# One layer of a streaming encoder: weights converted two tiles ahead, a norm's last squares summed on TensorE, a Silu behind the norm's statistics

## The chip, the cores and the metric

The kernel runs on one core of one Trainium2 chip. The core has five engines, each with a queue of its own that it works through strictly in order: TensorE (PE in the profile) for matmuls, VectorE (DVE), ScalarE (ACT), GpSimd (POOL) and SyncE (SP), which here only issues DMA transfers. They meet at semaphores. The metric is the device time of one execution in microseconds (us), lower is better. About 0.2% of it (some 3.5 us) is what a measurement of this kernel can tell from no change.

## What is computed

One layer of a hybrid encoder over 1024 new frames of one stream and 64 of another, width 1024, all in float32. Cut to what matters here (`x` is the residual stream, `mix` the result of the two head groups, `mod` six vectors made from a conditioning vector):

```python
mod = jax.nn.silu(c) @ w_ada + b_ada
sh1, sc1, gt1, sh2, sc2, gt2 = jnp.split(mod, 6, axis=-1)
...
mix = jnp.concatenate([y_rwkv, y_fox], axis=-1) @ w_out
x = x + gt1[:, None] * mix
h2 = _rms_norm(x, norm2_g) * (1 + sc2[:, None]) + sh2[:, None]
ffn = (jax.nn.silu(h2 @ w_ffn_gate) * (h2 @ w_ffn_up)) @ w_ffn_down
x = x + gt2[:, None] * ffn
```

`_rms_norm` divides by the root of the mean square over the 1024 columns of a frame.

## The kernel before

Activations lie with features on the 128 partitions and frames along the free axis, so a vector of 1024 features is 8 tiles (`KT`). Frames are split into two halves: half 0 has 512 frames, half 1 has 576 (512 and the 64 of the second stream), which is worked in two chunks of 288 columns. Each float32 product is made of three matmuls: weights and activations are each split into a rounded high part and a low rest (`whi`, `wlo`), and high by high, low by high and high by low are summed (`mm3`, L294 to L296).

A weight tile takes four steps: a DMA into one of four raw buffers (`raw_w`, L282), a cast to the high part on ScalarE (L212), a subtraction for the low part on VectorE (L216), and its matmuls. There are two buffers each for the high and the low part, so tile o+2 can be cast only when the matmuls of tile o are over.

The stage that the change touches is the stretch from the end of the attention to the first block of the feed-forward network, in `run`:

- The **output projection of half 1** (`outproj`): for each of 8 tiles o, 48 matmuls into the PSUM tile `po` (24 for each chunk), and VectorE adds the gated result to the residual `x1` (`add_gated`, L1002; three instructions for a tile, of 288, 224 and 64 columns, since the last chunk holds both streams).
- Behind each tile `x1_sq`: a DMA of the tile to a scratch tensor (L1008), its squares on ScalarE (L1010, into `nsq`, two buffers), and the sum with the squares so far on VectorE (L1012). At the end `x1_rs` sums over partitions with a matmul against ones (L1022, PSUM tile `pn2`) and forms the reciprocal root as Ln and Exp on ScalarE (L1025, L1026, into `nrs`).
- In between the tiles stand the steps of `h2_make` for half 0, a generator: the norm itself (L1050 on VectorE, L1052 on ScalarE), and the seven sums and differences of blocks of `h2` (L1054, L1055; `hh` and `hl`) that a Strassen-like feed-forward with seven products instead of eight needs. From o = 4 the first gate weights are loaded, at o = 5 prepared in the same way (`fast_prep`, L1096, L1100, L1106: `hS1` to `hS4`, `hA22` and their low parts).
- Then `x1_rs` of half 1, four tiles of the conditioning product (`ada_run`: 8 matmuls `pada`, a copy `mrow` on ScalarE, a transposing matmul, two small VectorE instructions each), and the feed-forward (`ffn`), whose first block runs the gate product of half 0 (`pfa`, `pfb`, `pfc`, `pfe` against `hh0`, 84 matmuls of 256 columns), with the steps of `h2_make` of half 1 between them, and then that of half 1 (against `hh1`). Its results go through Silu on ScalarE (L1198).

Code order is not the order on an engine. The kernel is written for a framework that lists each engine's instructions by a priority that follows the code, advances an instruction where its operands come free by its own reckoning, and adds the semaphores. A table of functions must be loaded on ScalarE (ACT_TABLE_LOAD) where the next function isn't in the loaded one; the loads are put in by the order of the instructions. The waits of an instruction hold up all that stands behind it on its engine.

Of the kernel before, what the change touches and what calls it, by code (L numbers as in the profile page):

```python
# [10 lines left out]
AF = mybir.ActivationFunctionType  # L11
# [5 lines left out]
P = 128  # L17
D = 1024
KT = D // P
# [45 lines left out]
class K:  # L65
# [938 lines left out]

    def x1_sq(self, hf, o, acc):

        nc, n = self.nc, hf.n
        nc.sync.dma_start(self.x1scr[hf.i][:, o], self.x1[hf.i][:, o, 0:n])  # L1008
        sq = self.slot(name="nsq", tag="hs")
        nc.scalar.activation(sq[:, 0:n], self.x1[hf.i][:, o, 0:n], AF.Square)  # L1010
        if acc is not None:
            nc.vector.tensor_tensor(sq[:, 0:n], sq[:, 0:n], acc[:, 0:n], op=ALU.add)  # L1012
        return sq

    def x1_rs(self, hf, acc):

        nc, n = self.nc, hf.n
        rs = self.slot(name="nrs", tag="rs")
        sums = []
        for off, m in hf.chunks:  # L1020
            ps = self.ps([P, 512], tag="b", name="pn2")
            nc.tensor.matmul(ps[:, 0:m], self.ones, acc[:, off:off + m], start=True, stop=True)  # L1022
            sums.append(ps)
        for a, (off, m) in zip(sums, hf.chunks):
            nc.scalar.activation(rs[:, off:off + m], a[:, 0:m], AF.Ln, scale=1.0 / D, bias=self.eps_n)  # L1025
        nc.scalar.activation(rs[:, 0:n], rs[:, 0:n], AF.Exp, scale=-0.5)  # L1026
        return rs
# [142 lines left out]
    def ffn(self, halves, raw, w, h2gen, gap, early, mid):  # L1170
# [3 lines left out]
        nc, A = self.nc, self.A  # L1174
# [3 lines left out]
        for i in range(len(src)):  # L1178
# [8 lines left out]
            for hf in halves:  # L1187
                n = hf.n // 2

                def out(q, ps, u):  # L1190
                    if not up:
# [3 lines left out]
                        if u is not None:  # L1195
                            nc.vector.tensor_tensor(d, ps, u, op=ALU.add)
                            ps = d
                        nc.scalar.activation(d, ps, AF.Silu)  # L1198
                        return
# [132 lines left out]
    def run(self):  # L1332
        tc, nc, A, O = self.tc, self.nc, self.A, self.O
        halves = [Half(0), Half(1)]
        with ExitStack() as top:
# [167 lines left out]
            acc = None  # L1503
            for o in range(KT):
                acc = self.x1_sq(halves[0], o, acc)
            w1 = [self.load_w(A["w_out"][o], [P, KT, P]) for o in range(2)]
            h2 = self.h2_make(halves[0], self.x1_rs(halves[0], acc))
            pair = lambda x: [A[x][i] for i in range(2)]
            acc, raw, w, ada = None, [], {}, []
            for o in range(KT):  # L1510
                self.outproj(halves[1], o, ("ab", "ce")[o % 2], w1[o] if o < 2 else None)
                acc = self.x1_sq(halves[1], o, acc)
                next(h2, None)
                if o in (0, 2):
                    next(h2, None)
# [7 lines left out]
            ada = [(t, self.ada_load(t)) for t in range(40, 44)]  # L1523
            rs = self.x1_rs(halves[1], acc)

# [176 lines left out]
```

## Time and profile before

| | us |
|---|---|
| time, median of 3 runs | 1743.63 |
| lowest and highest run | 1741.31, 1744.07 |
| the profiled execution's own time | 1735.94 |
| its span, first to last instruction | 1734.2 |
| PE busy in the span | 1663.8 (96%) |
| DVE busy | 1126.6 (65%) |
| ACT busy | 729.1 (42%) |

The mean granted TensorE clock is 0.981. All stretches below are of this one execution, in us from the first instruction: the output projection of half 1 lies at 925 to 988, the first block of the feed-forward from there to about 1045. In rows of the timeline stand start, duration, engine, source line, operation, written tile and read tiles, shape, how many instructions were merged, and in brackets the idle time of the engine just before it with what ended it. Durations of successive matmuls overlap; what a matmul costs is the distance of starts.

### The profile page before, as it was taken

How to read it: one execution, taken by the hardware profiler on the slowest of the kernel's cores; microseconds unless marked ns; L12 is line 12 of the kernel's file. 1: busy time of each engine (PE TensorE's matmuls, PEld its weight loads, DVE VectorE, ACT ScalarE, POOL GpSimd, SP SyncE). 2: the span in 40 equal slices, each digit the busy share in tenths (PEclk: the TensorE clock that was granted, in tenths of full speed). 3: DMA queues.
4: the chain of work that ended last, by engine and by line, in shares of the span. 5: the costliest groups of instructions: out<-in, count | busy, mean ns of one | idle time of the engine just before them, and what ended most of it. 6: DMA issues, size and time to landing. Idle time of an engine off the chain costs nothing.

```text
span 1734.2 us, 33257 instructions
## 1 busy us (share of the span) xinstructions
PE 1663.8 (96%) x12893; PEld 1447.9 (83%) x12893; DVE 1126.6 (65%) x2574; ACT 729.1 (42%) x1532; POOL 180.8 (10%) x412
## 2 busy tenths in 40 slices
PE   5999999999999999889999989999999999999999
PEld 3676766688888888766888889999999999999998
DVE  6676676757686753876877686666666655555545
ACT  4534454553454445765776453333233223211210
POOL 2102121131221212300210000000000000000000
PEclk9999999999899999989999999999999999999999
DMA  8535457632233344566553333222222224433213
GB/s 314 149 95 137 142 140 207 175 93 56 55 76 75 95 121 136 157 194 177 151 177 136 127 115 101 75 75 75 76 75 82 78 87 143 161 98 98 95 37 122
DMA packets 133581, 207.09 MB, mean 119 GB/s; under 512 B 62126, under 2 KB 70350, under 8 KB 133422
## 3 DMA queue, kind: packets, MB, share of 16 engines
q1 hardware_dynamic: 133422, 204.95, 39.3%
q8 instruction: 102, 1.67, 0.4%
q14 instruction: 57, 0.47, 0.1%
HBM read 157.65 MB, written 47.25 MB: 118 GB/s over the span
## 4 chain that ended last, share of the span: by engine, by line
PE 82%; DVE 7%; ACT 7%; DMA 2%; issue 2%; SPq 1%; POOL 0%; DVEq 0%; ACTq 0%; POOLq 0%
PE pd L1264 15%; PE pfc L1153 8%; PE pfe L1153 8%; PE pfa L1153 7%; PE pmm L294 5%; PE pmm L296 5%; PE pmm L295 5%; PE pfb L1153 4%; PE pav L962 2%; PE pbs L375 2%; PE pA L464 2%; PE ppt L940 2%; PE po L294 1%; PE po L295 1%; PE po L296 1%
## 5 line engine op out<-in xcount | busy, mean ns | idle before, releaser
L294 PE MATMUL pmm<-hhi,whi 128*128 128x288 f32 (+1 forms) x624 | 220.7, 354 | 0.7 <-ACT pb L317 0.7
L295 PE MATMUL pmm<-hlo,whi 128*128 128x288 f32 (+1 forms) x624 | 218.2, 350 | 0.0
L296 PE MATMUL pmm<-hhi,wlo 128*128 128x288 f32 (+1 forms) x624 | 218.0, 349 | 0.0
L212 ACT CAST whi<-wraw 128x1024 fp32r<-128x1024 f32 (+2 forms) x116 | 99.3, 856 | 214.4 <-PE pd L1264 167.0
L1264 PE MATMUL pd<-ah,wlo 128*128 128x512 f32 (+1 forms) x528 | 173.5, 329 | 0.0
L1264 PE MATMUL pd<-al,whi 128*128 128x512 f32 (+1 forms) x528 | 173.2, 328 | 0.0
L1264 PE MATMUL pd<-ah,whi 128*128 128x512 f32 (+1 forms) x528 | 173.0, 328 | 0.0
L1268 DVE SCALAR_TENSOR_TENSOR x1t<-pd,mod,x1t 128x512 f32<-128x512 f32 x192 | 91.4, 498 | 110.6 <-PE pd L1264 110.0
L294 PEld LDWEIGHTS pmm<-hhi,whi 128*128 128x128 f32 x624 | 120.3, 193 | 13.5 <-ACT pb L317 2.0
L296 PEld LDWEIGHTS pmm<-hhi,wlo 128*128 128x128 f32 x624 | 120.3, 193 | 10.9 <-issue 1.7
L295 PEld LDWEIGHTS pmm<-hlo,whi 128*128 128x128 f32 x624 | 120.4, 193 | 9.6 <-issue 0.7
L216 DVE TENSOR_TENSOR wlo<-wraw,whi 128x1024 fp32r<-128x1024 f32 (+2 forms) x108 | 103.8, 961 | 26.0 <-ACT whi L212 25.6
L1153 PE MATMUL pfc<-hh,hS 128*128 128x256 f32 (+1 forms) x352 | 102.0, 290 | 4.4 <-ACT hh L1055 4.4
L1264 PEld LDWEIGHTS pd<-al,whi 128*128 128x128 f32 x528 | 99.4, 188 | 7.7
L1264 PEld LDWEIGHTS pd<-ah,whi 128*128 128x128 f32 x528 | 99.3, 188 | 7.7
L1264 PEld LDWEIGHTS pd<-ah,wlo 128*128 128x128 f32 x528 | 99.2, 188 | 7.4
L1153 PE MATMUL pfc<-hl,hS 128*128 128x256 f32 (+1 forms) x352 | 102.3, 290 | 0.0
L1153 PE MATMUL pfc<-hh,lS 128*128 128x256 f32 (+1 forms) x352 | 102.0, 290 | 0.0
L1153 PE MATMUL pfa<-hl,whi 128*128 128x256 f32 (+1 forms) x352 | 101.8, 289 | 0.0
L1153 PE MATMUL pfa<-hh,whi 128*128 128x256 f32 (+1 forms) x352 | 101.7, 289 | 0.0
L1153 PE MATMUL pfa<-hh,wlo 128*128 128x256 f32 (+1 forms) x352 | 101.4, 289 | 0.0
L604 POOL TENSOR_SCALAR sd<-sv,pc 64x64 f32<-64x64 f32 x136 | 72.0, 529 | 172.9 <-DVE sv L617 156.6
(360 smaller groups left out, 4402.0 us busy)
## 6 DMA issues: line engine op xcount, KB each, us to landing
wraw<-in_w_in_dram SPq DMA_DIRECT2D x52, 512.0 KB
wada<-in_w_ada_dram SPq DMA_DIRECT2D x48, 512.0 KB
as<-actscr SPq DMA_DIRECT2D x22, 544.0 KB
wraw<-in_w_gate_dram SPq DMA_DIRECT2D x22, 512.0 KB
wraw<-in_w_up_dram SPq DMA_DIRECT2D x22, 512.0 KB
wraw<-in_w_down_dram SPq DMA_DIRECT2D x40, 256.0 KB
wraw<-in_w_out_dram SPq DMA_DIRECT2D x16, 512.0 KB
actscr<-sg SPq DMA_DIRECT2D x22, 288.0 KB
```

The source lines that it names most:

```text
L212: nc.scalar.copy(hi, src)
L216: eng.tensor_tensor(lo, src, hi.bitcast(F32), op=ALU.subtract)
L294: nc.tensor.matmul(ps[0:M, 0:n], whi[:, k, 0:M], xhi[:, k, off:off + n], start=(k == 0), stop=False)
L295: nc.tensor.matmul(ps[0:M, 0:n], whi[:, k, 0:M], xlo[:, k, off:off + n], start=False, stop=False)
L296: nc.tensor.matmul(ps[0:M, 0:n], wlo[:, k, 0:M], xhi[:, k, off:off + n], start=False, stop=(k == kt - 1))
L375: nc.tensor.matmul(ps[:, 0:n], w, x[:, off:off + n], start=True, stop=True)
L464: nc.tensor.matmul(pa[h][:, i], kb[hp, c + i], rk[hp, c + i], start=True, stop=True)
L604: nc.gpsimd.tensor_scalar(sd[hsl[h]], sv[hsl[h], c, h], pc[hsl[h], c], None, op0=ALU.mult)
L940: nc.tensor.transpose(pt[0:rows, b - b0, t * P:t * P + qn], p[0:qn, pc:pc + rows], self.ident[0:qn, 0:qn])
L1153: nc.tensor.matmul(ps, l[:, k], r[:, s, k], start=(first and k == 0 and y == 0), stop=(k == 3 and y == 2), skip_group_check=True)
L1264: nc.tensor.matmul(ps[:, 0:n], w[:, i], x[:, t:t + n], start=(i == 0 and y == 0), stop=(i == len(fs) - 1 and y == 2))
L1268: nc.vector.scalar_tensor_tensor(dst, ps[:, so - off:so - off + l], self.mod[:, 40 + o, b:b + 1], dst, op0=ALU.mult, op1=ALU.add)
```

## The change

Five things are changed in the stretch above; what is computed stays the same.

1. In half 1's projection the raw load, cast and subtraction of tile o+2 are issued right behind tile o, ahead of the norm's steps of half 0 that follow; before, tile o converted its own weights when its turn came (tiles 0 and 1 excepted).
2. Half 0's statistics and its first norm steps stand behind tile 1 instead of ahead of tile 0.
3. The squares of the last tile are made chunk by chunk and are not added to the sum on VectorE: `x1_rs` takes the sum of seven tiles and the last squares, and adds them up in PSUM, with two matmuls for each chunk.
4. The DMA of the last tile to scratch stands behind its squares in the code.
5. The Silus of the first gate block (`i == 0`, four for each half) are issued after the Exp of half 1's statistics.

```diff
-    def x1_sq(self, hf, o, acc):
+    def x1_sq(self, hf, o, acc, last=False):
         nc, n = self.nc, hf.n
+        sq = self.slot(name="nsq", tag="hs")
+        if last:
+            for off, m in hf.chunks:
+                nc.scalar.activation(sq[:, off:off + m], self.x1[hf.i][:, o, off:off + m], AF.Square)
         nc.sync.dma_start(self.x1scr[hf.i][:, o], self.x1[hf.i][:, o, 0:n])
-        sq = self.slot(name="nsq", tag="hs")
+        if last:
+            return sq
...
-    def x1_rs(self, hf, acc):
+    def x1_rs(self, hf, *accs):
...
-            nc.tensor.matmul(ps[:, 0:m], self.ones, acc[:, off:off + m], start=True, stop=True)
+            for i, acc in enumerate(accs):
+                nc.tensor.matmul(ps[:, 0:m], self.ones, acc[:, off:off + m], start=(i == 0), stop=(i == len(accs) - 1))
...
-        nc.scalar.activation(rs[:, 0:n], rs[:, 0:n], AF.Exp, scale=-0.5)
+        self.rs_done = nc.scalar.activation(rs[:, 0:n], rs[:, 0:n], AF.Exp, scale=-0.5)
...
-                        nc.scalar.activation(d, ps, AF.Silu)
+                        if i == 0:
+                            with self.tc.issue_after(self.rs_done.ins):
+                                nc.scalar.activation(d, ps, AF.Silu)
+                        else:
+                            nc.scalar.activation(d, ps, AF.Silu)
...
-            h2 = self.h2_make(halves[0], self.x1_rs(halves[0], acc))
+            acc0 = acc
...
-                self.outproj(halves[1], o, ("ab", "ce")[o % 2], w1[o] if o < 2 else None)
-                acc = self.x1_sq(halves[1], o, acc)
-                next(h2, None)
-                if o in (0, 2):
+                self.outproj(halves[1], o, ("ab", "ce")[o % 2], w1[o])
+                if o == KT - 1:
+                    sq = self.x1_sq(halves[1], o, None, True)
+                else:
+                    acc = self.x1_sq(halves[1], o, acc)
+                if o + 2 < KT:
+                    w1.append(self.load_w(A["w_out"][o + 2], [P, KT, P]))
+                if o == 1:
+                    h2 = self.h2_make(halves[0], self.x1_rs(halves[0], acc0))
+                    next(h2, None)
+                    next(h2, None)
+                if o:
+                    next(h2, None)
+                if o == 2:
                     next(h2, None)
...
-            rs = self.x1_rs(halves[1], acc)
+            rs = self.x1_rs(halves[1], acc, sq)
```

How this moves instructions is seen at three places. The first is VectorE's queue around the low part of the fourth weight tile (o = 3), `wlo_11848` before; `hl0` and `x1_0` belong to half 0's norm, `po` to the projection, `nsq` to the sum of squares. Before:

```order
L1002 SCALAR_TENSOR_TENSOR x1_1_11590<-po_11779,mod_160,x1_1_11590 128x288
L1012 TENSOR_TENSOR nsq_11765<-nsq_11765,nsq_11700 128x576
L1054 TENSOR_TENSOR hl0_11586<-x1_0_9536,hh0_11585 128x1024
L1050 SCALAR_TENSOR_TENSOR x1_0_9536<-x1_0_9536,g2_162,nrs_11641 128x512
L1054 TENSOR_TENSOR x1_0_9536<-x1_0_9536 128x4x256
L1002 SCALAR_TENSOR_TENSOR x1_1_11590<-po_11805,mod_160,x1_1_11590 128x224
L1002 SCALAR_TENSOR_TENSOR x1_1_11590<-po_11805,mod_160,x1_1_11590 128x64
L1054 TENSOR_TENSOR x1_0_9536<-x1_0_9536 128x4x256
L216 TENSOR_TENSOR wlo_11848<-wraw_11845,whi_11847 128x1024
```

After, where the same tile's low part is called `wlo_11763`:

```order
L1018 TENSOR_TENSOR nsq_11625<-nsq_11625,nsq_11621 128x512
L1002 SCALAR_TENSOR_TENSOR x1_1_11590<-po_11729,mod_160,x1_1_11590 128x224
L1002 SCALAR_TENSOR_TENSOR x1_1_11590<-po_11729,mod_160,x1_1_11590 128x64
L216 TENSOR_TENSOR wlo_11763<-wraw_11760,whi_11762 128x1024
L1018 TENSOR_TENSOR nsq_11756<-nsq_11756,nsq_11694 128x576
L1057 SCALAR_TENSOR_TENSOR x1_0_9536<-x1_0_9536,g2_162,nrs_11766 128x512 x6
L1002 SCALAR_TENSOR_TENSOR x1_1_11590<-po_11785,mod_160,x1_1_11590 128x288
```

The subtraction stood behind the evictions of tile 2 (`po_11779`, `po_11805`) and all eight norm steps; now it stands behind the eviction of tile 1 (`po_11729`) and ahead of all of them. On TensorE the matmuls of tiles 0 to 7 now follow each other with only half 0's `pn2` between; before, 18 of the 84 matmuls of the feed-forward's first product (`pfa`, `pfc`) stood among those of tiles 6 and 7.

The second place is ScalarE's queue at the end of the projection: the squares of the last tile (`nsq`), the norm's Ln and Exp (`nrs`), the first Silu (`sg`). Before:

```order
L1010 ACTIVATE nsq_12200<-x1_1_11590 128x576
L1198 ACT_TABLE_LOAD
L1198 ACTIVATE sg_12360<-pfa_12295 128x256
L1025 ACT_TABLE_LOAD
L1025 ACTIVATE nrs_12211<-pn2_12212,eps_n_154 128x288
L1025 ACTIVATE nrs_12211<-pn2_12214,eps_n_154 128x288
L1026 ACT_TABLE_LOAD
L1026 ACTIVATE nrs_12211<-nrs_12211 128x576
L193 COPY mrow_12228<-pada_12219 128x128
```

After:

```order
L1012 ACTIVATE nsq_12199<-x1_1_11590 128x288
L1107 CAST hS2_12071<-wraw_11991 128x512
L1032 ACTIVATE nrs_12211<-pn2_12212,eps_n_154 128x288
L1107 CAST hS4_12079<-wraw_11989 128x512
L193 COPY mrow_12230<-pada_12221 128x128
L1012 ACTIVATE nsq_12199<-x1_1_11590 128x288
L1032 ACTIVATE nrs_12211<-pn2_12215,eps_n_154 128x288
L1033 ACTIVATE nrs_12211<-nrs_12211 128x576
L193 COPY mrow_12241<-pada_12232 128x128
L1164 COPY fu_12310<-pfa_12297 128x256
```

Three table loads and a Silu are gone from between squares and Exp; the whole program has five table loads before and two after, the second of them now for the first Silu, 15 rows behind the Exp. Two casts of the gate's weights (`hS2`, `hS4`) and a copy of the conditioning product (`mrow`) have come in.

The third place is VectorE's queue at the same time. Before:

```order
L216 TENSOR_TENSOR wlo_12143<-wraw_12140,whi_12142 128x1024
L1012 TENSOR_TENSOR nsq_12135<-nsq_12135,nsq_12041 128x576
L1002 SCALAR_TENSOR_TENSOR x1_1_11590<-po_12146,mod_160,x1_1_11590 128x288
L1002 SCALAR_TENSOR_TENSOR x1_1_11590<-po_12172,mod_160,x1_1_11590 128x224
L1002 SCALAR_TENSOR_TENSOR x1_1_11590<-po_12172,mod_160,x1_1_11590 128x64
L1012 TENSOR_TENSOR nsq_12200<-nsq_12200,nsq_12135 128x576
L1050 SCALAR_TENSOR_TENSOR x1_1_11590<-x1_1_11590,g2_162,nrs_12211 128x512
```

After:

```order
L1002 SCALAR_TENSOR_TENSOR x1_1_11590<-po_12146,mod_160,x1_1_11590 128x288
L1103 TENSOR_TENSOR wraw_11991<-wraw_11991,wraw_11989 128x512
L1002 SCALAR_TENSOR_TENSOR x1_1_11590<-po_12172,mod_160,x1_1_11590 128x224
L1103 TENSOR_TENSOR wraw_11989<-wraw_11989,wraw_11991 128x512
L1103 TENSOR_TENSOR lS2_12072<-wraw_11991,hS2_12071 128x512
L1002 SCALAR_TENSOR_TENSOR x1_1_11590<-po_12172,mod_160,x1_1_11590 128x64
L1103 TENSOR_TENSOR lS4_12080<-wraw_11989,hS4_12079 128x512
L200 TENSOR_REDUCE mred_12244<-pada_12221 128x2
L201 TENSOR_SCALAR mod_160<-mred_12244,vc_135 128x2
L1057 SCALAR_TENSOR_TENSOR x1_1_11590<-x1_1_11590,g2_162,nrs_12211 128x512
```

The sum of the last squares (`nsq_12200`) is gone; the preparation of the gate's weights, which was over by then, now lies between the evictions of the last tile.

## The prediction

> **What bounds the kernel now.** First the page, for the whole span:
>
> ```profile
> span 1734.2 us, 33257 instructions
> PE 1663.8 (96%) x12893; PEld 1447.9 (83%) x12893; DVE 1126.6 (65%) x2574; ACT 729.1 (42%) x1532; POOL 180.8 (10%) x412
> PE 82%; DVE 7%; ACT 7%; DMA 2%; issue 2%; SPq 1%; POOL 0%; DVEq 0%; ACTq 0%; POOLq 0%
> ```
>
> TensorE bounds the program, and carries 82% of the chain that ended last; a change pays where TensorE stands still. So the second view is the table of stretches around the changed stage (busy time, count; the column behind POOL is the granted TensorE clock):
>
> ```profile
> 925.00:936.00 11.00, 9.97 (x73) 9.74 (x74) 7.55 (x12) 6.17 (x10) 0.00 (x0) 1.00 0.79 287
> 936.00:944.00 8.00, 8.00 (x57) 7.52 (x57) 7.16 (x14) 6.43 (x11) 0.00 (x0) 1.00 0.43 140
> 944.00:951.00 7.00, 4.07 (x28) 3.60 (x27) 6.90 (x10) 7.00 (x10) 0.00 (x0) 0.99 0.11 42
> 951.00:966.00 15.00, 15.00 (x103) 15.00 (x103) 13.52 (x18) 7.45 (x9) 0.00 (x0) 0.89 0.42 128
> 966.00:989.00 23.00, 21.07 (x160) 20.64 (x159) 15.38 (x25) 6.31 (x10) 0.00 (x0) 1.00 0.37 130
> 989.00:1012.00 23.00, 15.39 (x177) 12.64 (x175) 17.48 (x36) 22.16 (x40) 0.00 (x0) 0.93 0.44 151
> 1012.00:1030.00 18.00, 17.87 (x149) 17.23 (x148) 17.07 (x29) 9.02 (x16) 0.00 (x0) 0.90 0.16 59
> 1030.00:1460.00 430.00, 430.00 (x3427) 430.00 (x3427) 255.84 (x493) 130.89 (x245) 0.00 (x0) 1.00 0.25 81
> ```
>
> From 1030 TensorE has no gap, so what is won before shifts all the rest. Losses lie in two places: at 944 to 951, where DVE (6.90 of 7) and ACT (7.00) are full and TensorE waits, and at 989 to 1012, where ACT is busy 22.16 of 23 us. TensorE's timeline names the waits:
>
> ```profile
> 925.53 0.40 PE L294 MATMUL po<-mixrh,whi 128*128 128x288 f32 x1 [0.84 <-DVE x L1002]
> 935.81 1.13 PE L1022 MATMUL pn<-nsq,ones 128*128 128x512 f32 x2 [0.50 <-DVE nsq L1012]
> 939.97 0.29 PE L294 MATMUL po<-mixrh,whi 128*128 128x288 f32 x1
> 946.32 0.29 PE L294 MATMUL po<-mixrh,whi 128*128 128x288 f32 x1
> 947.64 0.40 PE L294 MATMUL po<-mixrh,whi 128*128 128x288 f32 x1 [0.62 <-ACT whi L212]
> 950.73 0.48 PE L296 MATMUL po<-mixrh,wlo 128*128 128x288 f32 x1 [2.31 <-DVE wlo L216]
> 971.92 0.40 PE L294 MATMUL po<-mixrh,whi 128*128 128x288 f32 x1 [1.35 <-ACT whi L212]
> 980.52 0.40 PE L294 MATMUL po<-mixrh,whi 128*128 128x288 f32 x1 [0.57 <-ACT whi L212]
> 987.59 0.30 PE L296 MATMUL po<-mixfh,wlo 128*128 128x288 f32 x1
> 1005.75 0.29 PE L1153 MATMUL pfa<-hh,wlo 128*128 128x288 f32 x1
> 1010.41 0.61 PE L1153 MATMUL pfc<-hh,hS 128*128 128x288 f32 x1 [4.37 <-ACT hh L1055]
> ```
>
> The projection's tile 2 starts at 939.97, tile 3 at 946.32: 48 matmuls without a wait take 6.35 us, 0.132 each. Its end T is 987.59 + 0.13 = 987.72. The next fixed point is 1010.41, the first matmul that waits 4.37 us for a block of half 1's norm; behind it TensorE hardly waits. Before, that point is T + 22.69.
>
> **Part 1: T.** In the changed order nothing but half 0's statistics stands among the 384 matmuls of half 1's projection. The first 7 (of the second chunk) fill the 0.84 us ahead of 925.53. From there: 41 matmuls of tile 0, 41 × 0.132 = 5.4; tile 1, 6.35; the statistics 1.1 (row 935.81); tiles 2 to 7, 6 × 6.35 = 38.1. T = 925.5 + 51.0 = 976.5, if no weights come late: 11.2 us earlier. The same from the other side: waits of 0.50, 0.62, 2.31, 1.35 and 0.57 (5.35 us), the half clock behind them (15 us at 0.89: 1.65), 18 feed-forward matmuls that move behind T (18 × 0.117, by 256 to 288 columns: 2.1), the 7 early ones (0.9); the other 1.2 I put down to tiles worked in pieces.
>
> Do the weights come in time? A tile's cast can start when tile o−2 is done, and tile o−1 then covers it for 6.35 us; cast and subtraction take 1.05 and 1.14 back to back (below). What else stands on DVE decides: it was busy 7.16 + 6.90 + 13.52 + 15.38 = 42.96 us from 936 to 989, and this work, less the 0.5 us by which tile 2's subtraction is now ahead, must fit between 936 and some 2.3 us behind T, 42.8 us. It just fits. **DVE has nothing to spare here**: I followed its new queue with the starts of these rows, and it comes to the last tile's evictions 0.2 us late, to the weights of tiles 4 to 7 1.5 to 3 us early. Bounds of its lateness: 0, and 3.5 us, which is what it idled in 925 to 936 (11 − 7.55), where half 0's squares and sums wait for each other, if as much comes back later. I take 0.7, nearer to the followed queue.
>
> At nothing I cost: the gate weights' loads, which now stand behind tile 1's and 2's scratch transfers and are wanted only near T; half 0's norm some 2 us later, since its blocks are wanted first behind T. Cover gone, each would show one for one on T.
>
> **Part 2: T to the feed-forward of half 1.** ACT and DVE rows of before:
>
> ```profile
> 988.60 0.69 ACT L1010 ACTIVATE nsq<-x 128x576 f32<-128x576 f32 x1 [7.29 <-DVE x L1002]
> 989.31 1.28 ACT L1198 ACT_TABLE_LOAD   x1
> 990.60 0.38 ACT L1198 ACTIVATE sg<-pfa 128x256 f32<-128x256 f32 x1
> 991.00 1.28 ACT L1025 ACT_TABLE_LOAD   x1
> 992.30 0.89 ACT L1025 ACTIVATE nrs<-pn,eps_n 128x288 f32<-128x288 f32 x2
> 993.20 1.28 ACT L1026 ACT_TABLE_LOAD   x1
> 994.50 0.68 ACT L1026 ACTIVATE nrs<-nrs 128x576 f32<-128x576 f32 x1
> ```
>
> ```profile
> 948.33 1.22 DVE L1054 TENSOR_TENSOR x<-x 128x1024 f32<-128x1024 f32 x1
> 949.46 1.22 DVE L216 TENSOR_TENSOR wlo<-wraw,whi 128x1024 fp32r<-128x1024 f32 x1
> 975.48 0.69 DVE L1096 TENSOR_TENSOR wraw<-wraw 128x512 f32<-128x512 f32 x1
> 976.08 0.69 DVE L1096 TENSOR_TENSOR lS<-wraw,hS 128x512 fp32r<-128x512 f32 x1
> 987.93 0.64 DVE L1002 SCALAR_TENSOR_TENSOR x<-po,mod,x 128x224 f32<-128x224 f32 x2 [2.42 <-PE po L296]
> 989.32 0.76 DVE L1012 TENSOR_TENSOR nsq<-nsq 128x576 f32<-128x576 f32 x1 [0.75 <-ACT nsq L1010]
> 995.21 0.75 DVE L1050 SCALAR_TENSOR_TENSOR x<-x,g,nrs 128x512 f32<-128x512 f32 x1 [5.13 <-ACT nrs L1026]
> ```
>
> Before, the first norm step stood at 995.21, T + 7.5. Between lay three table loads and a Silu (3 × 1.28 + 0.38 = 4.2 us; the sum of squares ran beside them). After, in us from T: eviction of 224 columns at 0.2; on DVE two gate preparations of 0.60 each (start to start 975.48, 976.08) stand ahead of the last 64 columns, which are done at 2.1. ACT meanwhile does the first Ln at 1.15, the casts and the copy, and is free at 2.4 to 2.5; squares of 288 columns 0.4 (half the 0.69 and a start) to 2.9; the closing matmul (row 935.81, 1.13 × 288/512 = 0.6) to 3.5; Ln 0.45 (row 992.30, one of two) and Exp 0.68: norm at 4.7. So 2.8 us of the 4.2 are won; the rest goes to the casts and the cut eviction. Bounds: 3.3 (7.5 − 4.2) and 7.5, nothing won.
>
> From the first norm step to 1010.41 are 15.2 us in which ACT is full. One table load stays in them, before and after. Added are the Silu (0.38) and a copy that had run earlier; gone are one `mrow` copy and short waits: + 0.1. The 66 remaining matmuls (18 more than before, 2.1 us) fit in TensorE's idle time, which was 4.37 us at the end alone. So T + 4.7 + 15.3 = T + 20.0 against T + 22.7: 2.7 us.
>
> The Trainium skill, "ScalarE: Activation LUTs" (section What ACT_TABLE_LOAD costs), gives a load some 1.28 us and a drain of 1.38 on top for each switch. Here the Silu at 990.60 starts 0.01 us behind the load's end at 990.59: the trace agrees with the load and shows no drain. By the page three loads would be 8.0 us and the gain 4.1 more; I go by the rows.
>
> **Sum.** 11.2 + 2.7 − 0.7 = 13.2 us. The profiled execution took 1735.94 us (span 1734.2), so 1722.7. The runs' median is 1743.63, 7.7 above that execution; I carry the gain over: 1743.63 − 13.2 = **1730.4 us**.
>
> **The rivals.**
>
> *DVE takes TensorE's place.* Full from 936 on, it reaches the last squares later than T + 2.3; each us of delay is one. For it: 42.4 of 42.8 us. Against: its queue has no wait for TensorE left but the evictions. Gain 6 to 11, about 1734.5. Chance 0.18.
>
> *The clock stays whole.* Before, TensorE idled from 1006 to 1010.41 and ran the next 18 us at 0.90, 1.8 us lost. After, TensorE runs out of half 0's product near T + 16.3 by the same following of queues (T + 18.1 before, row 1005.75) and idles 3.7 us; if that is too short to drop the clock, the gain is 15 to 17.5, about 1728. The shorter gap of 2.31 us at 950.73 was followed by 0.89, which speaks against it. The Trainium skill, "TensorE: Matmul & The Clock Gate" (section HAM oscillation), names idle gaps above some 3.4 us; the trace shows the clock falling behind a shorter one. Chance 0.09.
>
> *The gaps were covered anyway* (the change doesn't do what it says): the waits for `whi` and `wlo` return in the new order, and what is won on T is given back at half 1's norm, where ACT is full. Within 0.2% (3.5 us, about what a measurement can tell): 1740 to 1747. Against: the blocks of that norm start from T, nothing else. Chance 0.05; gains of 3.5 to 6 another 0.04.
>
> *Slower: conditioning weights late.* In the new TensorE queue `pada` of the third and fourth conditioning tile stand ahead of some 40 matmuls of half 0's product and, on DVE, their reductions ahead of norm steps; their loads now wait for the gate weights' buffer (free at T + 1.8) and for the first `pada` (a buffer is used again). Landing by the only such pair in view:
>
> ```profile
> 993.55 0.80 SPq L178 DMA_DIRECT2D wada<-in_w_ada_dram  x2
> 994.50:997.75 3.25, 1.00 0.88 316
> ```
>
> Two loads of 512 KB issued at 993.55 moved their 1.0 MB by 997.75, 4.2 us. From T + 2.6, with another transfer ahead, that is T + 7; DVE wants the result at T + 9.7, after some 1.5 us of `pada`, copy and transposition. Slack 1 us; beyond it each us costs one, and slower than before by 3.5 us needs a landing behind T + 24. Chance 0.04, with 1747 to 1752.
>
> **How the numbers follow.** Forecast (gain 11 to 15) 0.60, DVE 0.18, clock 0.09, covered 0.05, small gain 0.04, slower 0.04. Faster by over 0.2%: 0.60 + 0.18 + 0.09 + 0.04 = 0.91; same 0.05; slower 0.04. The range takes in the first three: from 1726 (gain 17.5) to 1738 (5.6).
>
> **What would show it.** Right: between 925 and the last `po` no wait of TensorE for `whi` or `wlo`, and 51 us from first to last; granted clock 1.00 there; one table load between the last squares and the first `hh` of half 1; first norm step 4.7 us behind T, and the wait for `hh` ending near T + 20. Wrong: DVE's evictions of the last tile late, `pada` waiting for a DMA, or a half clock in the first product, which would make its 66 matmuls late for DVE.

## The result, and the profile after

| | before | after |
|---|---|---|
| median of 4 runs each, us | 1742.87 | 1727.83 |
| lowest and highest run | 1741.31, 1744.07 | 1725.11, 1730.69 |
| profiled execution, span | 1735.94, 1734.2 | 1726.25, 1724.5 |
| mean granted clock | 0.981 | 0.979 |

The ratio of after to before is 0.992, with a 95% interval of 0.9898 to 0.9943: 14 us faster, between 10 and 18. The prediction was 1730.4.

The two profiled executions differ by less, 9.7 us, and that is no statement on the change. The program ahead of half 1's projection is the same in both, yet it took 3.25 us longer in the execution of after. So the traces are laid over each other at a point behind that: **H**, the start of the last 512-column matmul of half 0's projection (924.29 before, 927.54 after). From H to the end of the span it is 809.91 us before and 796.96 after: **12.95 us gained, where 13.2 were predicted.** T is the end of half 1's projection as in the prediction, and the "fixed point" its next one, the first feed-forward matmul that waits for half 1's norm.

First the page of after: the span, the busy times and the chain that ended last.

```profile
span 1724.5 us, 33263 instructions
PE 1666.6 (97%) x12897; PEld 1451.8 (84%) x12897; DVE 1124.9 (65%) x2573; ACT 725.7 (42%) x1530; POOL 179.7 (10%) x412
PE 83%; DVE 6%; ACT 5%; DMA 4%; issue 2%; SPq 0%; POOL 0%; DVEq 0%; ACTq 0%; POOLq 0%
```

TensorE works 2.8 us longer here than before, though half 1's projection has lost its waits: a busy sum mixes all stages, and those ahead of H took longer in this execution. The stretches tell more (busy time and count for PE, PEld, DVE, ACT, POOL, then the granted clock, DMA share, GB/s):

```profile
927.80:938.00 10.20, 10.20 (x78) 10.05 (x77) 7.80 (x12) 6.15 (x9) 0.00 (x0) 1.00 0.86 303
938.00:953.00 15.00, 15.00 (x111) 14.52 (x110) 13.26 (x22) 11.13 (x16) 0.00 (x0) 1.00 0.39 141
953.00:968.00 15.00, 15.00 (x115) 15.00 (x114) 14.82 (x22) 10.71 (x13) 0.00 (x0) 1.00 0.41 140
968.00:980.00 12.00, 12.00 (x92) 11.88 (x90) 11.86 (x17) 4.47 (x7) 0.00 (x0) 1.00 0.26 93
980.00:985.00 5.00, 5.00 (x54) 3.61 (x53) 3.15 (x9) 3.62 (x9) 0.00 (x0) 1.00 0.39 98
985.00:1001.00 16.00, 13.85 (x153) 12.19 (x151) 15.01 (x32) 14.92 (x29) 0.00 (x0) 1.00 0.69 252
1001.00:1020.00 19.00, 18.22 (x148) 17.21 (x149) 18.25 (x30) 10.22 (x19) 0.00 (x0) 0.91 0.16 56
1020.00:1450.00 430.00, 430.00 (x3427) 430.00 (x3426) 255.83 (x493) 131.17 (x246) 0.00 (x0) 1.00 0.25 81
```

The two losses of before read differently now. The first, 944 to 951 there, is gone: TensorE is full and at full clock from 927.8 to 985. DVE is full there instead (14.82 of 15, 11.86 of 12), without making TensorE wait. The second, 989 to 1012 there, is still here in 985 to 1001: ACT 14.92 of 16, DVE 15.01, TensorE 13.85. The timeline of TensorE has H, the last matmul of the projection (T = 979.56 + 0.13 = 979.69), and all three waits that are left between 920 and 1030:

```profile
927.54 0.39 PE L296 MATMUL po<-mixfh,wlo 128*128 128x512 f32 x1
979.56 0.30 PE L296 MATMUL po<-mixfh,wlo 128*128 128x288 f32 x1
989.16 0.64 PE L190 MATMUL pada<-wada,ct 128*32 128x128 f32 x16 [0.49 <-DMA wada<-in_w_ada_dram]
1000.92 0.40 PE L1160 MATMUL pfc<-hh,hS 128*128 128x288 f32 x1 [1.57 <-ACT hh L1062]
1001.97 0.40 PE L1160 MATMUL pfe<-hh,hS 128*128 128x288 f32 x1 [0.66 <-ACT hh L1062]
```

H to T is 52.15 us (63.43 before), T to the fixed point 21.23 (22.69), the fixed point to the end 723.58 (723.79). So the gain is 11.28 + 1.46 + 0.21. Why the middle part is smaller than the 2.7 predicted starts on DVE, behind T:

```profile
980.09 0.44 DVE L1002 SCALAR_TENSOR_TENSOR x<-po,mod,x 128x224 f32<-128x224 f32 x1
980.45 0.68 DVE L1103 TENSOR_TENSOR wraw<-wraw 128x512 f32<-128x512 f32 x1
981.05 0.68 DVE L1103 TENSOR_TENSOR lS<-wraw,hS 128x512 fp32r<-128x512 f32 x1
981.65 0.28 DVE L1002 SCALAR_TENSOR_TENSOR x<-po,mod,x 128x64 f32<-128x64 f32 x1
...
984.86 0.75 DVE L1057 SCALAR_TENSOR_TENSOR x<-x,g,nrs 128x512 f32<-128x512 f32 x1 [1.53 <-ACT nrs L1033]
...
990.97 0.17 DVE L200 TENSOR_REDUCE mred<-pada 128x2 f32<-128x8 f32 x1 [0.66 <-PE pada L198]
```

and on ACT:

```profile
982.32 0.45 ACT L1012 ACTIVATE nsq<-x 128x288 f32<-128x288 f32 x1
983.61 0.50 ACT L1032 ACTIVATE nrs<-pn,eps_n 128x288 f32<-128x288 f32 x1 [0.84 <-PE pn L1029]
984.14 0.69 ACT L1033 ACTIVATE nrs<-nrs 128x576 f32<-128x576 f32 x1
...
989.91 0.27 ACT L193 COPY mrow<-pada 128x128 f32<-128x128 f32 x1 [0.56 <-PE pada L190]
```

Two preparations of the gate's weights (L1103) lie between the last two evictions, so the last squares start 2.6 us behind T, and the first norm step (L1057) stands at T + 5.17. In the sixteen microseconds after that, all three engines stop once for one transfer: TensorE 0.49 for the fourth conditioning tile's weights, ACT 0.56 for its product, DVE 0.66 for its transposition. The chain of work that ended last names the transfer too (start, length, what):

```profile
982.65 6.37 DMA wada<-in_w_ada_dram
989.02 0.14 issue
989.16 0.64 PE pada L190 x16
```

### The profile page after: what moved, and what is told of

It is laid out like the page before. It is cut to its first block, busy times and chain, and to the rows that moved or that the text cites. A ratio compares the mean times of both kernels' runs of the same rounds, so it can differ in the third digit from the quotient of the medians.

```text
span 1724.5 us, 33263 instructions
## 1 busy us (share of the span) xinstructions
PE 1666.6 (97%) x12897; PEld 1451.8 (84%) x12897; DVE 1124.9 (65%) x2573; ACT 725.7 (42%) x1530; POOL 179.7 (10%) x412
## 4 chain that ended last, share of the span: by engine, by line
PE 83%; DVE 6%; ACT 5%; DMA 4%; issue 2%; SPq 0%; POOL 0%; DVEq 0%; ACTq 0%; POOLq 0%
PE pd L1275 15%; PE pfc L1160 8%; PE pfe L1160 8%; PE pfa L1160 8%; PE pmm L294 5%; PE pmm L296 5%; PE pmm L295 5%; PE pfb L1160 4%; PE pav L962 2%; PE ppt L940 2%; PE pbs L375 2%; PE po L295 2%; PE po L294 2%; PE po L296 2%; DMA wada<-in_w_ada_dram 2%; PE pA L464 2%
```

## Experiments

All measures are taken from H and T of each kernel's own trace, in us. H itself came between 922.96 and 933.83 us in these executions, at mean granted clocks between 0.974 and 0.982, with the same program ahead of it; a comparison of the spans alone would have drowned most of what follows. How fine the distances are: H to T is 63.40 to 63.43 in the three kernels with the order of before there, and 52.14 to 52.15 in five with that of after. Each kernel has one profiled execution, with its span given to 0.1 us, so a few tenths in the last two columns are not told from no difference.

| kernel | H to T | T to first norm step | T to fixed point | fixed point to end | H to end |
|---|---|---|---|---|---|
| before | 63.43 | 7.49 | 22.69 | 723.79 | 809.91 |
| after | 52.15 | 5.17 | 21.23 | 723.58 | 796.96 |
| e1_silu_alone | 63.40 | 4.94 | 23.11 | 724.15 | 810.66 |
| e11_silu_hold | 63.41 | 4.94 | 20.14 | 723.61 | 807.16 |
| e3_sum_back | 52.15 | 6.56 | 23.87 | 723.34 | 799.36 |
| e4_turn | 64.19 | 3.41 | 19.11 | 723.54 | 806.84 |
| e5_stat_first | 53.85 | 4.81 | 21.15 | 723.24 | 798.24 |
| e6_cond_late | 52.15 | 5.17 | 20.28 | 725.11 | 797.54 |
| e8_more_dve | 52.69 | 7.17 | 22.31 | 724.87 | 799.87 |
| e9_pool_lo | 52.32 | 9.47 | 25.49 | 723.57 | 801.38 |
| e12_fill | 52.14 | 5.18 | 21.27 | 723.69 | 797.10 |
| e13_prep_behind | 52.14 | 4.41 | 20.90 | 723.75 | 796.79 |

### Which part brings T: converting early (e4) or moving the statistics (e5)

```diff
 e4_turn, against after
-                self.outproj(halves[1], o, ("ab", "ce")[o % 2], w1[o])
+                self.outproj(halves[1], o, ("ab", "ce")[o % 2], w1[o] if o < 2 else None)
...
-                if o + 2 < KT:
-                    w1.append(self.load_w(A["w_out"][o + 2], [P, KT, P]))
```

> The changed kernel with change 1 undone: tile o converts its own weights when its turn comes; half 0's statistics and norm steps still stand behind tile 1, the last squares are still summed on TensorE, the Silu is still behind the Exp. T - H is 63.4 before and 52.2 after. Theory A (converting early removes the waits for the weights and the half clock behind them, some 7 to 9 of the 11.3 us): T - H 58 to 61, waits of 1 us and more for the high or low part of tiles 2 to 5. Rival B (it is the statistics' new place that frees ScalarE and VectorE when the weights want them; only the 18 feed-forward matmuls come back among the tiles, 2.1 us): T - H 53 to 55, no wait of 0.5 us for weights. Whole time over that of the changed kernel by the same differences, less what the feed-forward matmuls save behind T.

Measured: H to T 64.19, beyond even theory A's 58 to 61, and 0.76 longer than before. The waits of TensorE in its projection, summed (total, times, longest):

```profile
PE po L294 <- ACT whi L212: 4.2, 3, 2.4
PE po L296 <- DVE wlo L216: 3.0, 1, 3.0
```

The 7.2 us are more than the 4.8 of the same two kinds before. The timed ratio to before is 0.9972 (0.9949 to 0.9995): some 5 us of the 14 are left, and 3.07 from H to the end in the profiled execution. What is left is won behind T, where the fixed point comes sooner, at T + 19.11: with T this late, VectorE has the gate weights ready before the last evictions, and the first norm step stands at T + 3.41.

```diff
 e5_stat_first, against after
-            acc0 = acc
+            h2 = self.h2_make(halves[0], self.x1_rs(halves[0], acc))
...
-                if o == 1:
-                    h2 = self.h2_make(halves[0], self.x1_rs(halves[0], acc0))
-                    next(h2, None)
-                    next(h2, None)
-                if o:
-                    next(h2, None)
-                if o == 2:
+                next(h2, None)
+                if o in (0, 2):
                     next(h2, None)
```

> The changed kernel with change 2 undone: weights are still converted two tiles ahead, but half 0's statistics and first norm steps stand ahead of tile 0 as before. Theory A (early conversion alone removes the waits for weights): T - H 52.5 to 54.5 (52.2 after; the half microsecond for the statistics' matmul, which again stands close behind its sum, and the 0.9 us of early matmuls are what change 2 gave). Rival B (the statistics' place decides): waits for the weights of tiles 2 and 3 come back, T - H 57 or more.

Measured: 53.85, no wait for weights, and the two waits that change 2 removes are back, 0.84 for the residual ahead of tile 0 and 0.52 for the sum of squares. So early conversion is the cause of the shorter projection (12.04 us against e4), and moving the statistics is worth 1.70 there, 1.28 at the end. With conversion on its turn and everything else as in after (e4), the projection is 0.76 longer than before: moving the statistics gains nothing there without early conversion.

### The Silu and its table loads (e1, e11)

Change 5 moves nothing in the changed kernel: without it, the program is row for row the same on all five engines. The product's matmuls no longer run ahead of T, so no Silu is ready before the Exp, and the three table loads leave without being told to. Whether the prediction's 4.2 us are on the path can be tried only on the kernel of before.

```diff
 e1_silu_alone, against before
-        nc.scalar.activation(rs[:, 0:n], rs[:, 0:n], AF.Exp, scale=-0.5)
+        self.rs_done = nc.scalar.activation(rs[:, 0:n], rs[:, 0:n], AF.Exp, scale=-0.5)
...
-                        nc.scalar.activation(d, ps, AF.Silu)
+                        if i == 0:
+                            with self.tc.issue_after(self.rs_done.ins):
+                                nc.scalar.activation(d, ps, AF.Silu)
+                        else:
+                            nc.scalar.activation(d, ps, AF.Silu)
```

> The kernel before with change 5 alone: the Silus of the first gate block behind the Exp of half 1's statistics. H is the start of the last 512-column matmul of half 0's projection, T the end of half 1's projection, the fixed point the first feed-forward matmul that waits for a block of half 1's norm. Before: T - H = 63.4, T to the fixed point 22.7; after: 52.2 and 21.2. In the changed kernel change 5 moves no row, since the product's matmuls no longer run ahead of T and the Silu is not ready before the Exp anyway; so the prediction's 4.2 us of table loads and Silu can be tested only here. Theory (the loads and the Silu between squares and Exp are on the path): T - H stays 63.4, first norm step at T + 3.3 to T + 3.5 in place of T + 7.5, fixed point at T + 18.5 to T + 19.5, whole time 3 to 4 us below before. Rival (the sum of squares on VectorE and what stands behind it cover them): fixed point stays at T + 22 to T + 22.7, whole time within 1 us of before.

Measured: the first norm step 2.55 us earlier, not 4.2: ACT now waits 1.63 us for the sum over partitions, which the loads had covered. And of the 2.55 nothing arrived; the fixed point is 0.42 later than before, the time the same (ratio to before 0.9992, 0.9973 to 1.0011). Neither side of the expectation has this. ScalarE's timeline ahead of the fixed point (1017.15) shows the new wait:

```profile
1008.19 0.42 ACT L1200 ACTIVATE sg<-sg 128x256 f32<-128x256 f32 x1 [0.19 <-DVE sg L1196]
1010.88 1.04 ACT L1106 CAST whi<-wraw 128x1024 fp32r<-128x1024 f32 x1 [2.28 <-DMA wraw<-in_w_up_dram]
1011.84 1.81 ACT L1052 ACTIVATE x<-x,mod 128x512 f32<-128x512 f32 x4
```

With the Silu moved, the framework listed the first cast of the up-projection's weights ahead of four norm steps; in before it stands behind the fixed point, at 1011.77. The queue is in order, the transfer had not landed, and the norm waited behind a cast that only two matmuls of the next product wanted, listed ahead of the fixed point as well (TensorE waited 1.31 us for it at 1011.98, and 4.67 for the norm behind them). The next kernel holds that cast back:

```diff
 e11_silu_hold, against e1_silu_alone
-        nc.scalar.copy(hi, r1)
+        if hold:
+            with self.tc.issue_after(hold.ins):
+                nc.scalar.copy(hi, r1)
+        else:
+            nc.scalar.copy(hi, r1)
...
-                    gen = self.fast_prep(raw[1], nw)
+                    gen = self.fast_prep(raw[1], nw, self.tops[2])
```

> The kernel before with change 5 alone, as in the first experiment, and the first cast of the up-projection's weights held behind the cast of half 1's fifth block (the one of index 2). There the first norm step came 2.55 us earlier (T + 4.9 against T + 7.5), but the fixed point stood at T + 23.1 against T + 22.7 before: ScalarE's queue had that cast ahead of four norm steps, and it waited 2.28 us for the weights' transfer. Theory (that wait swallowed the gain): without it the first norm step is again at T + 4.9 and the fixed point at T + 20.0 to T + 20.8, T - H 63.4. Rival (TensorE's matmuls or VectorE's queue swallowed it): fixed point at T + 22 or later with the cast held as well.

Measured: T + 20.14, and 2.75 us from H to the end won against before. With the wait of 2.28 and the cast of 1.05 out of the norm's way, the gain arrives: they had swallowed it.

### Squares summed on TensorE (e3)

```diff
 e3_sum_back, against after
-                if o == KT - 1:
-                    sq = self.x1_sq(halves[1], o, None, True)
-                else:
-                    acc = self.x1_sq(halves[1], o, acc)
+                acc = self.x1_sq(halves[1], o, acc)
...
-            rs = self.x1_rs(halves[1], acc, sq)
+            rs = self.x1_rs(halves[1], acc)
```

> The changed kernel with change 3 and 4 undone: the last squares are made whole and added to the sum on VectorE, one matmul for each chunk. In its order 33 matmuls of half 0's product stand between the last matmul of the projection and the first sum over partitions. Theory (the sum on TensorE saves one step of the chain, about 0.8 us, of which VectorE's 0.76 us is the core): T - H 52.2 as in the changed kernel, first norm step at T + 6.0 to T + 6.5 in place of T + 5.2, fixed point at T + 22.0 to T + 22.5 in place of T + 21.2. Rival (the conditioning weights, which land at T + 9.3, set the fixed point): first norm step later, the fixed point within 0.3 us of T + 21.2. Second rival (the 33 matmuls ahead of the sum over partitions decide): first norm step at T + 7 or later, fixed point at T + 23 or later.

Measured: first norm step at T + 6.56, 1.39 later than after (the theory had 0.8 to 1.3). The experiment undoes changes 3 and 4 together, but change 4 moves no row: with the transfer issued ahead of the squares, each engine of the changed kernel has the same instructions in the same order. So the 1.39 belong to change 3 and the order that comes with it. The fixed point is 2.64 later, where only the second rival had it, but not for that rival's reason: from norm to fixed point it took 17.31 us in place of 16.06, and in them ScalarE again had the cast of the up-projection's weights ahead of the last two norm steps, 1.14 us of waiting for the transfer and 1.05 of work (in after it stands behind the fixed point, at 1002.27). So summing the last squares on TensorE saves 1.4 us at the norm; the rest belongs to an order that came with it.

### Is VectorE full (e8, e9)

```diff
 e8_more_dve, against after
-                    w1.append(self.load_w(A["w_out"][o + 2], [P, KT, P]))
+                    raw2 = self.raw_w(A["w_out"][o + 2], [P, KT, P])
+                    w1.append(self.split_w(raw2, [P, KT, P]))
+                    if o in (3, 4):
+                        wh2, wl2 = w1[-1]
+                        nc.vector.tensor_tensor(wl2, raw2, wh2.bitcast(F32), op=ALU.subtract)
```

> The changed kernel with the subtraction that makes the low part done twice for tiles 5 and 6 (two more VectorE instructions of 1.14 us, the same result). Theory (VectorE is full from 943 us to the last squares, so what is added to it comes out behind T one for one): T - H within 0.3 us of 52.2, first norm step at T + 7.0 to T + 7.6 in place of T + 5.2, fixed point 1.5 to 2.3 us later. Rival 1 (it has slack): first norm step within 0.4 us of T + 5.2. Rival 2 (its lateness reaches TensorE at once): waits for the low parts return and T - H is 53.5 or more.

Measured: 2.28 us more work on DVE put T 0.54 and the first norm step 2.00 us later behind it, 2.54 together. There is no slack, and the lateness comes out close to one for one; that T moves too was not expected to this size, and one small wait (0.28) for a low part is back. The fixed point is 1.08 later behind T, less than the 1.5 expected, and the end 2.91 later from H.

```diff
 e9_pool_lo, against after
+                    self.pool_lo = o in (2, 3, 4, 5)
                     w1.append(self.load_w(A["w_out"][o + 2], [P, KT, P]))
+                    self.pool_lo = False
```

> The changed kernel with the subtractions for the low parts of tiles 4 to 7 on GpSimd, which stands still in this stretch; on GpSimd one took 2.38 us elsewhere in the program, on VectorE 1.14. VectorE is relieved of 4.6 us. Theory (VectorE's queue, with the gate weights' preparation between the last evictions, is what puts the first norm step at T + 5.2; with conversion on its turn and the preparation over it stood at T + 3.4): first norm step at T + 3.4 to T + 4.2, fixed point at T + 19.2 to T + 20.2 if the conditioning weights come no later, T - H 52.2. Rival (the freed time goes to other work that the framework now lists earlier, and the same rows stay between the evictions): first norm step within 0.4 us of T + 5.2. Second rival (GpSimd's subtractions come late for the matmuls or slow VectorE beside them): waits for low parts, T - H over 53.

Measured: first norm step at T + 9.47, 4.30 later, though DVE was relieved. TensorE did not wait for the low parts (H to T 52.32), so of the second rival only the slower VectorE came. GpSimd's rows, and what stood on DVE beside the first two of them:

```profile
953.71 2.41 POOL L216 TENSOR_TENSOR wlo<-wraw,whi 128x1024 fp32r<-128x1024 f32 x1 [22.98 <-ACT whi L212]
961.43 2.40 POOL L216 TENSOR_TENSOR wlo<-wraw,whi 128x1024 fp32r<-128x1024 f32 x1 [5.31 <-ACT whi L212]
```

```profile
953.79 2.88 DVE L1057 SCALAR_TENSOR_TENSOR x<-x,g,nrs 128x512 f32<-128x512 f32 x1
956.59 1.21 DVE L1061 TENSOR_TENSOR x<-x 128x1024 f32<-128x1024 f32 x1
...
961.64 3.28 DVE L1061 TENSOR_TENSOR x<-x 128x1024 f32<-128x1024 f32 x1
```

A norm step that takes 0.75 us elsewhere took 2.88, a difference of blocks that takes 1.21 took 3.28. The kinds of instruction on DVE that read two tensors from SBUF took 8 us more over 41 us (7 low parts of half 0's blocks 10.6 in place of 8.4, 4 differences 8.6 in place of 4.9, 8 norm steps 7.7 in place of 5.5), against the 4.9 that left. The Trainium skill, "SBUF — State Buffer" (section SBUF: two separate sides), says that GpSimd and a DVE instruction with two SBUF inputs share one pair of ports, which the first to start holds for its whole length. The trace agrees: GpSimd's rows end at 956.12 and 963.83, the stretched ones at 956.67 and 964.92, about their own length later.

### The conditioning weights (e6)

```diff
 e6_cond_late, against after
-                ada_run(ada[4:])
+                ada_run(ada[3:])
...
-            ada_run(ada)
+            ada_run(ada[:3])
```

> The changed kernel with the fourth of the four conditioning tiles moved from ahead of half 0's first product to the gap behind it, where the next four stand anyway. In the changed kernel TensorE waited 0.49 us for this tile's weights, which landed at T + 9.3, ScalarE then 0.56 for its product and VectorE 0.66; the first norm step stood at T + 5.2 and the fixed point (first feed-forward matmul that waits for half 1's norm) at T + 21.2. Theory (these late weights are what puts 16.1 us instead of the predicted 15.3 between norm and fixed point): no wait for that load ahead of the norm's steps, first norm step unchanged, fixed point at T + 20.2 to T + 20.6. Rival (ScalarE, busy 14.9 of 16 us there, is the bound, and takes up the freed time elsewhere): fixed point at T + 20.9 to T + 21.4.

Measured: first norm step unchanged, fixed point at T + 20.28, 0.95 earlier: the theory's size, though the tile's own work on ACT and DVE went with its late weights. But the program ends 0.58 later from H. The tile's matmuls (0.64 and 0.27 us) went from a TensorE that has gaps to one that has none; the fixed point to the end is 1.53 longer. The 0.6 us above those matmuls I have not followed.

### The preparation between the last evictions (e13), and the clock (e12)

```diff
 e13_prep_behind, against after
-                    for _ in self.fast_prep(raw[0], w):
-                        pass
+                    prep0 = self.fast_prep(raw[0], w)
+                    for _ in range(4):
+                        next(prep0)
...
             rs = self.x1_rs(halves[1], acc, sq)
+            for _ in prep0:
+                pass
```

> The changed kernel with the preparation of the first gate weights issued in two parts: its first four steps where they stood, the rest behind half 1's statistics. On VectorE the two last evictions of the projection then follow each other, with the preparation behind them; in the changed kernel two preparations of 0.6 us stood ahead of the last 64 columns, and the first norm step at T + 5.2. Theory (that queue sets the first norm step): it comes at T + 3.7 to T + 4.3, the fixed point at T + 19.6 to T + 20.6, T - H 52.2; whole time 0.5 to 2 us below the changed kernel, that is 14 to 17 us below before. Rival (the preparation is only moved from ahead of the norm into it, where VectorE and ScalarE are full as well): first norm step as in the theory but the fixed point at T + 21 or later, whole time within 0.4 us of the changed kernel. Second rival (the product of half 0 wants these weights at once): waits of TensorE for the gate's weights ahead of the fixed point.

Measured: first norm step at T + 4.41, 0.76 earlier (the theory had 0.9 to 1.5), of which 0.33 reached the fixed point and 0.17 the end; the time is that of after (ratio to before 0.9918, 0.9894 to 0.9943). The rival holds nearest: what leaves the place ahead of the norm goes into it.

```diff
 e12_fill, against after
-                    nc.tensor.matmul(ps, l[:, k], r[:, s, k], start=(first and k == 0 and y == 0), stop=(k == 3 and y == 2),
-                                     skip_group_check=True)
+                    mm = nc.tensor.matmul(ps, l[:, k], r[:, s, k], start=(first and k == 0 and y == 0),
+                                          stop=(k == 3 and y == 2), skip_group_check=True)
+                    if fill and (x, k, y) in ((0, 3, 2), (2, 0, 0)):
+                        with self.tc.issue_after(mm.ins):
+                            for _ in range(8 if x == 0 else 0):
+                                nc.tensor.matmul(self.fill, wh[:, 0] if x == 0 else w["A11"][0][:, 0], bh[:, 0, 0, 0:224],
+                                                 start=True, stop=True, skip_group_check=True)
...
+                if x == 0:
+                    self.fill = full[:, 288:512]
```

> The changed kernel with eight more matmuls (224 columns, into columns of a PSUM bank that nothing reads, so the result is the same) behind half 1's first twelve feed-forward matmuls, where TensorE waited 1.57 us ahead of the fixed point; the rest of its order is unchanged. They take some 0.85 us, so TensorE's longest idle stretch there falls to about 0.7 us, beside the 0.66 us behind it. In the changed kernel the granted clock was 0.66 in the five us behind the fixed point, 1.7 us lost. Theory (the clock falls by how long TensorE stands still in one stretch): clock above 0.9 there, fixed point to the end of the program 722.0 to 722.6 us in place of 723.6. Rival (it falls whenever a stretch is not full, or at a phase that has nothing to do with this idle): clock 0.6 to 0.75 again, fixed point to end 723.3 to 723.9; T - H and T to the fixed point (52.2 and 21.2) unchanged in both.

Measured: TensorE's stretches in e12 from the fixed point (997.91) on, the clock in the third column from the right:

```profile
993.91:997.91 4.00, 3.37 (x36) 2.92 (x35) 4.00 (x5) 4.00 (x7) 0.00 (x0) 1.00 0.47 133
997.91:1002.91 5.00, 4.35 (x29) 3.95 (x30) 5.00 (x5) 3.73 (x6) 0.00 (x0) 1.00 0.00 2
1002.91:1007.91 5.00, 4.49 (x57) 3.74 (x56) 5.00 (x9) 2.00 (x4) 0.00 (x0) 1.00 0.18 52
```

The clock stays whole with idles of 0.63 and 0.65 us, as the theory says. But that doesn't show the theory, for two other kernels have the same idle and different clocks. The waits at the fixed point, and the four microseconds ahead of it and five behind it, in e5 and then in e9:

```profile
1003.86 0.40 PE L1160 MATMUL pfc<-hh,hS 128*128 128x288 f32 x1 [1.29 <-ACT hh L1062]
999.86:1003.86 4.00, 2.71 (x36) 2.21 (x34) 3.86 (x5) 4.00 (x7) 0.00 (x0) 1.00 0.59 193
1003.86:1008.86 5.00, 4.30 (x27) 3.70 (x28) 5.00 (x5) 3.73 (x6) 0.00 (x0) 1.00 0.15 57
1008.63 0.40 PE L1160 MATMUL pfc<-hh,hS 128*128 128x288 f32 x1 [1.29 <-ACT hh L1062]
1004.63:1008.63 4.00, 2.71 (x36) 2.21 (x34) 4.00 (x5) 4.00 (x7) 0.00 (x0) 1.00 0.61 197
1008.63:1013.63 5.00, 4.34 (x19) 4.08 (x20) 5.00 (x5) 3.72 (x6) 0.00 (x0) 0.66 0.14 54
```

After 1.29 us each, with TensorE equally busy ahead, the clock is 1.00 in e5 and 0.66 in e9. So the length of one idle doesn't settle it at this size, and the rival, a phase that has nothing to do with the idle, stays open; e12 may owe its whole clock to either. The theory's price is refuted: the same first `pfb` of a later product stands 36.83 us behind the fixed point in after and 36.09 in e12 (1037.75 and 1034.00 in the two timelines). That is 0.74 us, not 1.7: DVE is full in all three stretches, and TensorE, faster, has gaps (4.49 of 5 busy in the third row, where after had 4.91). And at the end even this is gone, at a wait that after doesn't have:

```profile
1453.85 0.40 PE L1163 MATMUL pfe<-hh,hA 128*128 128x288 f32 x1 [0.59 <-DVE fu L1222]
```

## Why the prediction was right

- **T, 11.2 us: right, and for the reason given.** 11.28 measured; no wait for `whi` or `wlo`, clock 1.00, and e4 shows that without early conversion nothing of it is left. The 1.2 us that the second way of adding up put down to tiles worked in pieces were not followed.
- **VectorE with nothing to spare, 0.7 us late: right in kind.** The 0.7 us that the sum took off were not lost at T; VectorE's lateness comes out behind it. e8 gives the slope: 2.28 us more work, 2.54 us later.
- **Part 2, 2.7 us: the mis-sized term, 1.46.** Two pieces of it. The norm came at T + 5.17 and not 4.7: the last squares ended at T + 3.1 (reckoned 2.9), and the second sum over partitions kept ACT waiting 0.84 where I put 0.6, so that the second Ln began at T + 3.9 (3.5). And from norm to fixed point it took 16.06 and not 15.3, because the fourth conditioning tile landed at T + 9.3 where the prediction had the loads at T + 7. I took the rate of two loads that ran alone, 4.2 us; here the load was issued at 982.65 (T + 3.0; reckoned T + 2.6), but it was one of five issued between 981.76 and 986.66, and took 6.37 us while the DMA engines were 95% busy. The rival "conditioning weights late" thus occurred, as 0.8 us; e6 gives 15.11 without that tile, its weights and its small work. The two parts also weigh on each other: with conversion on its turn (e4) Part 2 brings 3.58, with it early 1.46, since VectorE then does the gate's preparation between the last evictions.
- **The three table loads and the Silu, 4.2 us: right that they go, silent about why.** The prediction doesn't say which of the five changes removes them; the one that speaks of Silus moves no row, and it is change 1 that puts the product's matmuls behind T (with it undone, in e4, 18 of them stand ahead of T again). And the 4.2 us were worth 2.55 at the norm, since the sum's wait lay under them (e1).
- **The idle ahead of the fixed point, 3.7 us: wrong, 1.57.** The prediction counts 66 matmuls between the first norm step and the fixed point, 18 more than before's 48. In after's trace there are 84, 36 more: before had done 48 of half 0's by its first norm step, after only 12. The 18 that were not counted are 2.1 us at 0.117 each, which is the difference. It cost nothing here, since ScalarE set the fixed point. The idle was still followed by a half clock, 0.66 over five microseconds, as in before (0.50 after 4.37 us); as the clock can also stay whole after so short an idle (e5), it is in part luck that the rival of a whole clock did not come true. The rival that priced a whole clock at 1.8 us and more was mis-priced: 0.74 by e12, and none at the end.
- **The sum, 13.2 against 12.95: closer than its terms.** Part 2 brought 1.24 less than forecast, and the 0.7 taken off for VectorE at T was not lost there; the two errors in part cancel. The change in the last stretch, 0.21, is too small to be read.

What stays open: the fixed point of e13 was not followed beyond the observation that DVE and ACT are full, and what sets the clock behind a short idle is not shown. None of the kernels made from these readings ends more than 0.2 us earlier than after, counted from H.

## What to carry to other kernels

When weights are converted on their turn, the conversion stands behind whatever side work was issued since; issuing it one buffer's lifetime ahead takes it off TensorE's path even on an engine that is full, as long as the side work is not needed at once. In an in-order queue every cast of a later transfer is a possible wait: when a change frees time on an engine, look at what was advanced into it, and whether its data are there. Compare two traces from the last point that both programs share, not from the start.

## What the runs showed of the hardware

- A half clock can follow much shorter idles than before's 4.37 us: in the five microseconds behind the fixed point it was 0.66 after 1.29 us (e9) and after 1.57 (after), 0.72 after 1.94 (e6), 0.53 after 2.75 (e8); it was 1.00 after 0.63 (e12), and also after 1.29 (e5). The Trainium skill, "TensorE: Matmul & The Clock Gate" (section HAM oscillation), speaks of gaps above some 3.4 us; here the measurement decides: no single bound on one idle fits e5 and e9.
- GpSimd's subtraction of 128x1024 costs DVE some 2 us each time, more than the 1.2 us that it takes over from it.
- The same instructions ahead of H took from 922.96 to 933.83 us, a spread of 1.2%. The three executions with the lowest mean granted clock (0.974 to 0.976) have H at 930.6 to 933.8, the five at 0.981 and 0.982 at 923.0 to 928.9.
